# Layer 1's folded ConvFFN: seven-product pairs in a fixed order, with the next pair's weights made between the products

## The chip, the cores and the metric

The kernel runs on one core of one Trainium2 chip. A core has TensorE (PE in the profile, with its weight loads shown as PEld), VectorE (DVE), ScalarE (ACT), GpSimd (POOL) and SyncE (SP), each with an instruction stream of its own that it works through in order; DMA queues are fed from SP and POOL. The metric is the device time of one execution in microseconds (us), as the median over several runs. Lower is better.

## The reference

A decoder trunk of two layers on x of 512 tokens by 1024 channels, in float32. Each layer has a token mixer (layer 0: retention with 4 heads, layer 1: mLSTM with 4 heads) and then a ConvFFN; each of them works on a normed and modulated h and is added to the residual x under a gate. The part that matters here is the ConvFFN:

```python
def causal_dwconv(x, w, b):
    ...
    out = b + xp[:, 0:S] * w[0]
    for j in range(1, K):
        out = out + xp[:, j:j + S] * w[j]

def conv_ffn(h, w_up, conv_w, conv_b, w_down):
    u = causal_dwconv(h @ w_up, conv_w, conv_b)
    a, b = jnp.split(u, 2, axis=-1)
    return (jax.nn.silu(a) * b) @ w_down
```

h is 512 x 1024, w_up 1024 x 5632, the convolution has 3 taps, a and b are 2816 wide each, and w_down is 2816 x 1024.

## The kernel before

Everything is kept with channels on the 128 partitions and the 512 tokens along the free dimension, so x is 8 tiles of 128 x 512 and h likewise. To get float32 accuracy, every operand is split into a high part (a rounded copy, type fp32r) and a low part (what is left over), and each product is three matmuls: high by high, high by low, low by high. For a weight tile of 128 x 1024 (8 k-blocks of 128 columns) the high part is a cast on ACT (`high_part`, L153) and the low part a subtraction on DVE (`low_part`, L158). `low_part_added` makes the low part in another way: ACT writes the negated high part (L164), and a DMA issued from POOL adds the raw weights to it in flight (L165).

Work is listed as `items`, each with the weight chunks that it uses. A planner at the end of the kernel goes through the items in order, and makes chunks (load, high part, low part) up to AHEAD = 4 items ahead, as long as the sum of tiles that are held stays within BUDGET = 20. The wide tiles come from a pool of NWT = 23 slots, and the 128 x 512 tiles from a pool of NSLOTS = 56. Beyond that, a scheduler of the framework fixes the order of the instructions on each engine when the program is built, with the order of the source as priority; on the chip each engine then keeps that order.

The ConvFFN of a layer (class `Ffn`) works on 22 blocks f of 128 channels of a and the same of b. A plain block is two `proj_item`s, 24 matmuls of 512 columns each. The results go through `conv` (ACT and DVE), the gate (silu, product), and a split into the pair `gg`. The down-projection comes in groups of blocks, [4, 4, 4, 4, 6] for layer 1; a group of 4 has 4 pieces of two output tiles, 12 matmuls of 512 columns a tile, and `add_residual` (L377) adds each tile to x. The last group is worked in two halves of 256 tokens (`boundary`), beside the squares for the final norm.

In layer 1 the blocks f = 3 to 21 are folded: the 1024 x 256 weights of a block's pair and h are taken as 2 x 2 blocks (the a and b weights, the two halves of the 8 k-blocks; the two halves of the tokens), and the product is made with seven block products in place of eight (a scheme of Winograd's). `Start.sums` and `Start.turn` make the sums of h once, for all folds. `Fold` makes the sums of the weights of one pair: of the loaded tiles a and b come s13 (two sums on POOL, L187 and L189) and s24 (two on DVE, L188 and L190), then high and low parts of a, s13, s24 and of one half of b (`bp`, L199 and L200). `fold_item` runs the seven products, each 12 matmuls of 256 columns (L315 to L317), into the banks px and py, and combines them: ACT copies three partial results to SBUF (L320, L322, L324), POOL adds two of them there (L325, L328), and three additions on DVE write PSUM (L327, L331, L332). A `Fold` counts 8 tiles in the planner's budget, and each fold is one item; the down pieces of a group stand as items of their own, two after a fold, once the group's blocks are done.

Of the kernel before, what the change touches and what calls it, by code (L numbers as in the profile page):

```python
# [9 lines left out]
F32 = mybir.dt.float32  # L10
# [5 lines left out]
P = 128  # L16
# [11 lines left out]
NWT = 23  # L28
BUDGET = 20
# [8 lines left out]
NSLOTS = 56  # L38
# [30 lines left out]
def trunk(ctx: ExitStack, tc: tile.TileContext, xT, cb, pos, vec, decay, zmask, ada, w_s0, w_in0, w_v0,  # L69
# [107 lines left out]
    class Fold:  # L177


        tiles = 8  # L180

        def __init__(self, src, n, off):
            a, b, s13, s24 = (wide(uid(s)) for s in ("wa", "wb", "ws", "wt"))
# [3 lines left out]
            G.tensor_tensor(f(s13, 0), f(b, 0), f(b, 1), op=ALU.add)  # L187
            V.tensor_tensor(f(s24, 0), f(s13, 0), f(a, 0), op=ALU.subtract)  # L188
            G.tensor_tensor(f(s13, 1), f(a, 0), f(b, 0), op=ALU.subtract)  # L189
            V.tensor_tensor(f(s24, 1), f(a, 1), f(s24, 0), op=ALU.subtract)  # L190
            r = slice(0, n)
# [6 lines left out]
            bp = wide(uid("wb"), F32R)[:, off : off + n]  # L198
            A.copy(f(bp, 0), f(b, 1))  # L199
            V.tensor_tensor(f(bp, 1), f(b, 1), f(bp, 0).bitcast(F32), op=ALU.subtract)  # L200
            self.p = {1: (ah, 0, al, 0), 2: (ah, T, al, T), 3: (s24h, T, s24l, T), 4: (bp, 0, bp, T),
                      5: (s13h, 0, s13l, 0), 6: (s24h, 0, s24l, 0), 7: (s13h, T, s13l, T)}
# [100 lines left out]
    def fold_item(srcs, h, terms, thens):  # L303

        def fn(w):
            p, x_, y_ = w[0].p, bank("px"), bank("py")
            s, q = slot("fs"), slot("fq")

            def product(i, o, start):
# [8 lines left out]
            product(1, x_[:, HA], True)  # L318
            product(6, y_[:, HA], True)
            A.copy(s[:, HA], x_[:, HA])  # L320
            product(5, x_[:, HB], False)
            A.copy(s[:, HB], y_[:, HA])  # L322
            product(7, y_[:, HA], False)
            A.copy(q[:, HA], x_[:, HB])  # L324
            G.tensor_tensor(q[:, HA], q[:, HA], s[:, HA], op=ALU.add)  # L325
            product(2, x_[:, HA], False)
            V.tensor_tensor(y_[:, HB], y_[:, HA], q[:, HA], op=ALU.add)  # L327
            G.tensor_tensor(s[:, HB], s[:, HB], s[:, HA], op=ALU.add)  # L328
# [6 lines left out]
        item([Use(srcs, KT * P, Fold, OFF)], fn)  # L335
# [43 lines left out]
    def contract_tiles(w, n, gate, ys, i, t0, t1, after=lambda m: None):  # L379

        r = slice(t0, t1)
        per = WCOLS // (n * P)
        for j in range(per):
            m = i * per + j
            ps = bank("po")
            for k in range(n):
                cs = slice((j * n + k) * P, (j * n + k) * P + P)
                mm3(ps[:, r], w.hi[:, cs], w.lo[:, cs], ys(k).hi[:, r], ys(k).lo[:, r], k == 0, k == n - 1)
            add_residual(ps, m, gate(m), t0, t1)
            after(m)  # L390

    def pieces(src, n, gate, ys):
# [3 lines left out]
        def piece(i):  # L396
            def run(w, t0, t1, after=lambda m: None):
                contract_tiles(w, n, gate, ys, i, t0, t1, after)
            return Use(src(i), per * n * P), run
# [293 lines left out]
    class Ffn:  # L693
# [31 lines left out]
        def up(self, f):  # L725
            th, w = self.pair(f), w_up[self.layer]
            if self.folded and f > 2:
                fold_item((w[f], w[f + FT]), self.h, self.start.terms, (th, th))
            else:
                proj_item(w[f], self.h, th)  # L730
                proj_item(w[f + FT], self.h, th)
# [6 lines left out]
        def items(self, norm):  # L738
            groups = GROUPS[self.layer]
            if self.folded:  # L740
                ready, gi, end = [], 0, groups[0]
                for f in range(2, FT):
                    self.up(f)
                    if f == 2:
                        item([], lambda w: self.start.turn())
                    if f > end and gi < len(groups) - 1:
                        ready += self.down(gi)
                        gi += 1
                        end += groups[gi]
                    contract_items(ready[:2])  # L750
                    ready = ready[2:]
                contract_items(ready)
# [400 lines left out]
    at, held = 0, []  # L1153
    for n, (uses, fn, free) in enumerate(items):
        held = [u for u in held if u.last >= n]
        while at < len(flat) and (flat[at].first <= n + AHEAD) and (
                sum(u.kind.tiles for u in held) + flat[at].kind.tiles <= BUDGET):
# [3 lines left out]
        fn([u.chunk for u in uses])  # L1161
# [107 lines left out]
```

## Time and profile before

| | |
|---|---|
| median of 3 runs | 1622.29 us (1620.37 to 1623.98) |
| the profiled execution | 1618.41 us, its span 1616.6 us |
| PE busy | 1549.6 us, 96% |
| DVE busy | 1147.1 us, 71% |
| ACT busy | 763.1 us, 47% |
| POOL busy | 265.8 us, 16% |
| mean granted clock of TensorE | 0.988 |

The span runs from the first to the last instruction. A busy time is the time in which an engine had an instruction in work; PE's matmuls overlap, so that the distance between their starts says more than their durations. In rows of groups the columns are line, engine, operation, output and input tiles, shapes and count, then busy us and mean ns of one, then the idle time of the engine just before and what ended it. In rows of waits they are who waited, for whom, us in total, times, longest. In a timeline they are start and duration in us, with idle time before the instruction in brackets. The folded blocks lie between 1262 and 1580 us of the span, and the last down group follows to 1606.

### The profile page before, as it was taken

How to read it: one execution, taken by the hardware profiler on the slowest of the kernel's cores; microseconds unless marked ns; L12 is line 12 of the kernel's file. 1: busy time of each engine (PE TensorE's matmuls, PEld its weight loads, DVE VectorE, ACT ScalarE, POOL GpSimd, SP SyncE). 2: the span in 40 equal slices, each digit the busy share in tenths (PEclk: the TensorE clock that was granted, in tenths of full speed). 3: DMA queues.
4: the chain of work that ended last, by engine and by line, in shares of the span. 5: the costliest groups of instructions: out<-in, count | busy, mean ns of one | idle time of the engine just before them, and what ended most of it. 6: DMA issues, size and time to landing. Idle time of an engine off the chain costs nothing. (4 is left out here: it accounts for less than half of the span.)

```text
span 1616.6 us, 21716 instructions
## 1 busy us (share of the span) xinstructions
PE 1549.6 (96%) x8500; PEld 1340.9 (83%) x8500; DVE 1147.1 (71%) x1616; ACT 763.1 (47%) x1147; POOL 265.8 (16%) x266
## 2 busy tenths in 40 slices
PE   7899999999899999999999999999999798998997
PEld 4688888888888887788988888888898688988887
DVE  8975776777787677763676776757579676776866
ACT  4434524344453243441464554545434656656554
POOL 4221010200110000000110111010204143424322
PEclk9999999999999999999999999999999899999999
DMA  9344446443245655333214232312223455656551
GB/s 364 120 150 142 149 146 214 156 169 127 92 145 175 210 188 182 119 102 104 93 65 131 91 105 66 117 66 91 79 69 79 128 131 148 178 153 170 146 146 52
DMA packets 65304, 216.52 MB, mean 134 GB/s; under 512 B 8993, under 2 KB 11297, under 8 KB 65202
## 3 DMA queue, kind: packets, MB, share of 16 engines
q1 hardware_dynamic: 59730, 195.22, 36.1%
q0 software_dynamic: 5472, 19.93, 6.7%
q8 instruction: 66, 1.08, 0.3%
q14 instruction: 36, 0.29, 0.1%
HBM read 193.06 MB, written 2.12 MB: 121 GB/s over the span
## 5 line engine op out<-in xcount | busy, mean ns | idle before, releaser
L158 DVE TENSOR_TENSOR wlo<-raw,whi 128x1024 fp32r<-128x1024 f32 (+1 forms) x220 | 268.9, 1225 | 84.5 <-ACT whi L153 82.3
L215 PE MATMUL pp<-hh,wlo 128*128 128x512 f32 x800 | 312.4, 390 | 2.7 <-DVE wlo L158 2.7
L213 PE MATMUL pp<-hh,whi 128*128 128x512 f32 x800 | 311.4, 389 | 1.0 <-DVE vl L210 1.0
L214 PE MATMUL pp<-hl,whi 128*128 128x512 f32 x800 | 311.4, 389 | 0.0
L153 ACT CAST whi<-raw 128x1024 fp32r<-128x1024 f32 (+1 forms) x220 | 223.9, 1028 | 77.8 <-DMA raw<-w_in 29.9
L215 PEld LDWEIGHTS pp<-hh,wlo 128*128 128x128 f32 x800 | 150.2, 188 | 37.8 <-DVE wlo L158 6.9
L213 PEld LDWEIGHTS pp<-hh,whi 128*128 128x128 f32 x800 | 150.1, 188 | 32.0 <-DVE vl L210 1.4
L214 PEld LDWEIGHTS pp<-hl,whi 128*128 128x128 f32 x800 | 150.2, 188 | 31.0
L377 DVE SCALAR_TENSOR_TENSOR x<-po,mod,x 128x512 f32<-128x512 f32 (+1 forms) x168 | 102.6, 619 | 91.7 <-PE po L215 91.1
L213 PE MATMUL po<-ggh,whi 128*128 128x512 f32 (+1 forms) x464 | 155.7, 338 | 2.1 <-ACT ggh L209 1.9
L215 PE MATMUL po<-ggh,wlo 128*128 128x512 f32 (+1 forms) x464 | 155.8, 337 | 0.7 <-DVE wlo L158 0.6
L214 PE MATMUL po<-ggl,whi 128*128 128x512 f32 (+1 forms) x464 | 155.8, 337 | 0.0
L215 PE MATMUL po<-yh,wlo 128*128 128x256 f32 (+1 forms) x352 | 116.3, 333 | 3.9 <-DVE wlo L158 3.9
L213 PE MATMUL po<-yh,whi 128*128 128x256 f32 (+1 forms) x352 | 116.6, 332 | 0.8 <-ACT whi L153 0.8
L214 PE MATMUL po<-yl,whi 128*128 128x256 f32 (+1 forms) x352 | 116.4, 331 | 0.0
L130 DVE SCALAR_TENSOR_TENSOR ada<-ada,c_ext 128x1025 f32<-128x1025 f32 x93 | 114.6, 1237 | 0.0
L213 PEld LDWEIGHTS po<-ggh,whi 128*128 128x128 f32 x464 | 87.1, 189 | 12.3 <-ACT ggh L209 2.8
L315 PE MATMUL px<-hh,whi 128*128 128x256 f32 x304 | 87.5, 288 | 9.1 <-ACT whi L153 7.4
L215 PEld LDWEIGHTS po<-ggh,wlo 128*128 128x128 f32 x464 | 87.1, 188 | 10.8 <-DVE wlo L158 1.5
L214 PEld LDWEIGHTS po<-ggl,whi 128*128 128x128 f32 x464 | 87.3, 188 | 8.8
L317 PE MATMUL px<-hh,wlo 128*128 128x256 f32 x304 | 86.8, 286 | 7.4 <-DMA wlo<-wa 7.4
L708 DVE SCALAR_TENSOR_TENSOR cv<-pp,vecs,cv 128x511 f32<-128x511 f32 (+1 forms) x84 | 62.4, 748 | 43.7 <-ACT cv L706 42.6
(285 smaller groups left out, 3420.6 us busy)
## 6 DMA issues: line engine op xcount, KB each, us to landing
ada<-ada SPq DMA_DIRECT2D x96, 512.5 KB, 3.8
raw<-w_in SPq DMA_DIRECT2D x62, 512.0 KB, 3.4
raw<-w_up SPq DMA_DIRECT2D x50, 512.0 KB, 3.3
raw<-w_o SPq DMA_DIRECT2D x32, 512.0 KB, 3.5
raw<-w_dn SPq DMA_DIRECT2D x32, 512.0 KB, 3.4
raw<-w_v SPq DMA_DIRECT2D x28, 512.0 KB, 3.3
wa<-w_up SPq DMA_DIRECT2D x19, 512.0 KB, 3.2
wb<-w_up SPq DMA_DIRECT2D x19, 512.0 KB, 5.4
```

Source lines behind the costliest of these rows:

```text
L130: return V.scalar_tensor_tensor(raw, raw, 1.0, c_ext[:], op0=ALU.mult, op1=ALU.mult, accum_out=mods[layer][:, f : f + 1])
L153: A.copy(hi, w[:, r])
L158: V.tensor_tensor(lo, w[:, r], hi.bitcast(F32), op=ALU.subtract)
L213: PE.matmul(o, ah, bh, start=start, stop=False)
L214: PE.matmul(o, ah, bl, start=False, stop=False)
L215: PE.matmul(o, al, bh, start=False, stop=stop)
L315: PE.matmul(o, hi[:, ch], b[0], start=st, stop=False, skip_group_check=True)
L317: PE.matmul(o, lo[:, cl], b[0], start=False, stop=sp, skip_group_check=True)
L377: V.scalar_tensor_tensor(x[m][:, r], ps[:, r], gate_col, x[m][:, r], op0=ALU.mult, op1=ALU.add)
L708: V.scalar_tensor_tensor(acc[:, s:], ps[:, : T - s], c(j), acc[:, s:], op0=ALU.mult, op1=ALU.add)
```

## The change

The folds begin at f = 4, so block 3 is plain. PE's instructions within a fold item keep the order of the source (`manual_schedule`). The products' results are kept in two banks, c1 and c2: products 1, 6 and 7 are accumulated in one place of c2, with a copy taken after each, and product 5 starts c1's second half; POOL has no part in the combination any more. The weight sums s13 move from POOL to DVE. The weights of fold i + 1 are made in four steps that stand between the products of fold i (`step_a`: high and low of a, and the sums; `step_b`: s13; `step_c`: s24, its low part by DMA for odd folds and by DVE for even ones; `step_d`: the half of b), and the loads of fold i + 2 stand at its end. Folds 1 to 16 have a down piece each, its two tiles before and after product 7; folds 0 and 17 have none, and another order. Of the limits, NWT becomes 22, NSLOTS 58, BUDGET 16, or 20 while a fold is held, and a `Fold` counts 7.

```diff
-NWT = 23
-BUDGET = 20
+NWT = 22
+BUDGET = 16
+BUDGET_FOLD = 20
+FOLD_FROM = 4
...
-NSLOTS = 56
+NSLOTS = 58
...
     class Fold:
-        tiles = 8
+        tiles = 7
...
+        def load(self, src):
+            self.a, self.b = wide(uid("wa")), wide(uid("wb"))
+            nc.sync.dma_start(self.b[:, :WCOLS], src[1])
+            nc.sync.dma_start(self.a[:, :WCOLS], src[0])
+            self.p = {}
+
+        def both(self, w, low, i, j):
+            r = slice(0, WCOLS)
+            hi = high_part(w, r, OFF)
+            lo = low(w, hi, r, OFF)
+            self.p[i], self.p[j] = (hi, 0, lo, 0), (hi, T, lo, T)
+
+        def step_a(self):
+            a, b = self.a, self.b
             f = lambda t, i: t[:, i * T : i * T + T]
-            nc.sync.dma_start(a[:, :n], src[0])
-            nc.sync.dma_start(b[:, :n], src[1])
-            G.tensor_tensor(f(s13, 0), f(b, 0), f(b, 1), op=ALU.add)
+            self.s13, self.s24 = wide(uid("ws")), wide(uid("wt"))
+            s13, s24 = self.s13, self.s24
+            self.both(a, low_part_added, 1, 2)
+            V.tensor_tensor(f(s13, 0), f(b, 0), f(b, 1), op=ALU.add)
+            V.tensor_tensor(f(s13, 1), f(a, 0), f(b, 0), op=ALU.subtract)
             V.tensor_tensor(f(s24, 0), f(s13, 0), f(a, 0), op=ALU.subtract)
-            G.tensor_tensor(f(s13, 1), f(a, 0), f(b, 0), op=ALU.subtract)
             V.tensor_tensor(f(s24, 1), f(a, 1), f(s24, 0), op=ALU.subtract)
-            ah = high_part(a, r, off)
-            al = low_part_added(a, ah, r, off)
-            s24h = high_part(s24, r, off)
-            s24l = low_part(s24, s24h, r, off)
-            s13h = high_part(s13, r, off)
-            s13l = low_part_added(s13, s13h, r, off)
...
+        def step_b(self):
+            self.both(self.s13, low_part_added, 5, 7)
+
+        def step_c(self, added):
+            self.both(self.s24, low_part_added if added else low_part, 6, 3)
+
+        def step_d(self):
+            bp = wide(uid("wb"), F32R)[:, OFF : OFF + WCOLS]
+            A.copy(bp[:, :T], self.b[:, T:WCOLS])
+            V.tensor_tensor(bp[:, T:], self.b[:, T:WCOLS], bp[:, :T].bitcast(F32), op=ALU.subtract)
+            self.p[4] = (bp, 0, bp, T)
...
-            product(1, x_[:, HA], True)
-            product(6, y_[:, HA], True)
-            A.copy(s[:, HA], x_[:, HA])
-            product(5, x_[:, HB], False)
-            A.copy(s[:, HB], y_[:, HA])
-            product(7, y_[:, HA], False)
-            A.copy(q[:, HA], x_[:, HB])
-            G.tensor_tensor(q[:, HA], q[:, HA], s[:, HA], op=ALU.add)
-            product(2, x_[:, HA], False)
-            V.tensor_tensor(y_[:, HB], y_[:, HA], q[:, HA], op=ALU.add)
-            G.tensor_tensor(s[:, HB], s[:, HB], s[:, HA], op=ALU.add)
-            product(3, x_[:, HB], False)
-            product(4, y_[:, HA], False)
-            V.tensor_tensor(x_[:, HB], x_[:, HB], s[:, HB], op=ALU.add)
-            V.tensor_tensor(y_[:, HA], y_[:, HA], s[:, HA], op=ALU.add)
-            thens[0](x_)
-            thens[1](y_)
+            def u2():
+                A.copy(s[:, HB], c2[:, HA])
+                V.tensor_tensor(c1[:, HA], c1[:, HA], s[:, HA], op=ALU.add)
+
+            def u3():
+                A.copy(q[:, HA], c2[:, HA])
+                V.tensor_tensor(c2[:, HB], c1[:, HB], q[:, HA], op=ALU.add)
+            product(1, c2[:, HA], True)
+            if down:
+                product(5, c1[:, HB], True)
+                A.copy(s[:, HA], c2[:, HA])
+                prepare[0]()
+                product(2, c1[:, HA])
+                product(6, c2[:, HA])
+                u2()
+                prepare[1]()
+                down[1](w[1], 0, T, js=(0,))
+                product(7, c2[:, HA])
+                u3()
+                prepare[2]()
+                down[1](w[1], 0, T, js=(1,))
+            else:
+                product(2, c1[:, HA], True)
+                A.copy(s[:, HA], c2[:, HA])
+                prepare[0]()
+                product(6, c2[:, HA])
+                u2()
+                prepare[1]()
+                product(5, c1[:, HB])
+                product(7, c2[:, HA])
+                u3()
+                prepare[2]()
+            product(4, c2[:, HA])
+            product(3, c1[:, HB])
+            prepare[3]()
+            V.tensor_tensor(c1[:, HB], c1[:, HB], s[:, HB], op=ALU.add)
+            thens[0](c1)
+            thens[1](c2)
+            prepare[4]()
...
+                def steps(i):
+                    if i >= len(folds):
+                        return [lambda: None] * 4
+                    return [folds[i].step_a, folds[i].step_b, lambda: folds[i].step_c(i % 2), folds[i].step_d]
...
+                first = [load(0)] + steps(0) + [load(1)]
...
+                early(first[0])
+                self.up(2, lambda: None)
+                early(first[1])
+                th = self.pair(3)
+                proj_item(w[3], self.h, th)
+                early(first[2], first[3])
+                proj_item(w[3 + FT], self.h, th)
+                early(self.start.turn, first[4], first[5])
+                downs = [p for gi in range(len(groups) - 1) for p in self.down(gi)]
+                for i, fold in enumerate(folds):
+                    th = self.pair(FOLD_FROM + i)
+                    fold_item(fold, self.h, self.start.terms, (th, th), downs.pop(0) if i and downs else None,
+                              steps(i + 1) + [load(i + 2)])
...
+    def limit(held):
+        return BUDGET_FOLD if any(u.kind is Fold for u in held) else BUDGET
...
-        fn([u.chunk for u in uses])
+        with tc.manual_schedule(engines={mybir.EngineType.PE}) if any(u.kind is Fold for u in uses) else ExitStack():
+            fn([u.chunk for u in uses])
```

More of the change, by code (lines that the diff above doesn't have):

```diff
@@ L740, in items, with load, fn, early @@
             if self.folded:
[L741 to L752, printed above, removed]
+                w = w_up[self.layer]
+                folds = [Fold(None, 0, 0) for _ in range(FOLD_FROM, FT)]
+                def steps(i):
+                    if i >= len(folds):
+                        return [lambda: None] * 4
+                    return [folds[i].step_a, folds[i].step_b, lambda: folds[i].step_c(i % 2), folds[i].step_d]
+                def load(i):
+                    def fn():
+                        if i < len(folds):
+                            folds[i].load((w[FOLD_FROM + i], w[FOLD_FROM + i + FT]))
+                    return fn
+                first = [load(0)] + steps(0) + [load(1)]
+                def early(*fs):
+                    item([], lambda w: [f() for f in fs])
+                early(first[0])
[11 more added lines that the diff above has]
+                              steps(i + 1) + [load(i + 2)])
+                assert not downs
                 boundary([], self.down(len(groups) - 1), norm)
```

36 lines of the change are left out of this document (14 added, 22 removed).

## The prediction

> **What bounds the kernel now.** I read the page first, then busy time by stretch, then TensorE's (PE's) waits, then the start times of its matmuls.
>
> ```profile
> span 1616.6 us, 21716 instructions
> PE 1549.6 (96%) x8500; PEld 1340.9 (83%) x8500; DVE 1147.1 (71%) x1616; ACT 763.1 (47%) x1147; POOL 265.8 (16%) x266
> ```
>
> The profiled execution took 1618.41 us, 1.8 more than its span and 3.9 less than the median of the runs, 1622.29.
>
> ```profile
> core 0: us, PE busy (x) PEld busy (x) DVE busy (x) ACT busy (x) POOL busy (x), PEclk, DMA share, GB/s
> 0.00:1250.00 1250.00, 1218.11 (x6167) 1032.70 (x6168) 894.89 (x1247) 552.37 (x830) 146.44 (x146) 0.99 0.40 133
> 1262.00:1295.00 33.00, 22.86 (x150) 20.96 (x148) 21.34 (x33) 20.21 (x33) 7.13 (x7) 0.84 0.47 120
> 1295.00:1580.00 285.00, 269.62 (x1908) 251.38 (x1909) 198.98 (x279) 167.30 (x243) 101.69 (x100) 0.99 0.59 152
> 1580.00:1606.00 26.00, 25.75 (x218) 25.24 (x218) 14.71 (x30) 13.10 (x29) 6.05 (x8) 1.00 0.00 1
> ```
>
> PE bounds every stretch. The folded ConvFFN of layer 1 runs from 1262 to 1606, and its first 33 us have 10.1 us of PE idle. VectorE (DVE) is busy for 220.3 us of 318, ScalarE (ACT) for 187.5. The waits of PE from 1262 to 1606:
>
> ```profile
> PE px L315 <- ACT whi L153: 7.4, 1, 7.4
> PE px L317 <- DMA wlo<-wa: 7.4, 4, 3.5
> PE py L315 <- ACT whi L153: 5.6, 3, 1.9
> PE po L213 <- ACT ggh L209: 1.9, 2, 1.0
> PE py L317 <- DVE wlo L158: 1.5, 2, 0.8
> PE px L315 <- ACT fs L320: 1.4, 3, 0.7
> ```
>
> Together 25.2 us, nearly all for weights of a fold that are not ready. Start times show what else is lost:
>
> ```profile
> 1251.05 0.40 PE L213 MATMUL pp<-hh,whi 128*128 128x512 f32 x1
> ...
> 1261.73 0.39 PE L215 MATMUL pp<-hh,wlo 128*128 128x512 f32 x1
> 1261.95 0.28 PE L315 MATMUL px<-hh,whi 128*128 128x256 f32 x1
> ...
> 1275.19 0.58 PE L315 MATMUL px<-hh,whi 128*128 128x256 f32 x1 [7.42 <-ACT whi L153]
> ...
> 1278.33 0.41 PE L315 MATMUL px<-hh,whi 128*128 128x256 f32 x1
> ...
> 1280.67 0.41 PE L317 MATMUL px<-hh,wlo 128*128 128x256 f32 x1
> ...
> 1298.71 0.28 PE L315 MATMUL px<-hh,whi 128*128 128x256 f32 x1
> ...
> 1301.30 0.28 PE L316 MATMUL px<-hl,whi 128*128 128x256 f32 x1
> ...
> 1341.53 0.38 PE L317 MATMUL px<-hh,wlo 128*128 128x256 f32 x1 [1.09 <-DMA wlo<-wa]
> ...
> 1342.90 0.28 PE L316 MATMUL py<-t24l,whi 128*128 128x256 f32 x1
> ...
> 1605.62 0.28 PE L215 MATMUL po<-ggh,wlo 128*128 128x256 f32 x1
> ```
>
> A 512-column matmul starts every (1261.73 - 1251.05)/47 = 0.2272 us. A 256-column one starts every (1301.30 - 1298.71)/22 = 0.1177, but (1280.67 - 1278.33)/11 = 0.2127 after the 7.42 us gap: half speed. After a gap of 1.09 us it is (1342.90 - 1341.53)/11 = 0.125, not half. So a long stall is paid twice.
>
> From 1261.95 to 1605.62 PE does 19 folds x 84 matmuls of 256 columns, 16 down pieces x 24 of 512, and the last group, 8 tiles x 18 matmuls x 2 halves of 256: 1596 x 0.1177 + 384 x 0.2272 + 288 x 0.1177 = 187.8 + 87.2 + 33.9 = 308.9 us. The stretch takes 343.7. **The loss before is 34.8 us**: 25.2 in the waits above, the rest mostly half speed. That is all the change can win in this stage.
>
> **The change part by part.**
>
> *One fold fewer (FOLD_FROM is 4).* Block 3 goes as two plain projections, 48 x 0.2272 = 10.9 us, in place of 84 x 0.1177 = 9.9: **+1.0 us** on PE.
>
> *Sums on DVE, results added in PSUM.*
>
> ```profile
> L189 POOL TENSOR_TENSOR ws<-wa,wb 128x512 f32<-128x512 f32 x17 | 24.7, 1453 | 0.0
> L187 POOL TENSOR_TENSOR ws<-wb 128x512 f32<-128x512 f32 x17 | 24.3, 1430 | 14.5 <-DMA wb<-w_up 14.5
> L158 DVE TENSOR_TENSOR wlo<-wt,whi 128x1024 fp32r<-128x1024 f32 x17 | 21.3, 1251 | 7.6 <-ACT whi L153 7.6
> L188 DVE TENSOR_TENSOR wt<-ws,wa 128x512 f32<-128x512 f32 x17 | 18.0, 1059 | 5.6 <-POOL ws L187 5.6
> L153 ACT CAST whi<-wa 128x1024 fp32r<-128x1024 f32 x17 | 17.8, 1046 | 0.0
> L190 DVE TENSOR_TENSOR wt<-wa,wt 128x512 f32<-128x512 f32 x17 | 12.6, 743 | 0.2
> L322 ACT COPY fs<-py 128x256 f32<-128x256 f32 x19 | 7.1, 373 | 0.0
> L327 DVE TENSOR_TENSOR py<-py,fq 128x256 f32<-128x256 f32 x19 | 8.2, 430 | 25.7 <-PE py L317 16.9 <-POOL fq L325 5.9 <-POOL fs L328 2.9
> ```
>
> DVE gains 18 x 2 sums of 0.743 (26.7 us) and loses 10 of 19 low parts of the difference tile (12.5): 9 folds now take them by DMA, one fold is gone. L188, the same shape as L190 yet 0.32 us longer, should fall to its time with POOL's sums gone (18 x 0.32 = 5.7). So DVE is busy 220 + 26.7 - 12.5 - 5.7 = 229 us of about 300, ACT about 187 + 9 negations at the cast's 1.05 less the dropped fold's three such = 194. Both lie beside PE: nothing on the path while their queues are in time. The two partial-result additions of POOL go, the three ACT copies and three DVE additions stay; POOL keeps DMA issues alone.
>
> *The order of PE fixed.* One fold with a down piece takes, from its start: products 1, 5, 2, 6 to 5.65 us, a down tile to 8.38, product 7 to 9.79, a down tile to 12.52, products 4 and 3 to 15.34 (1.41 a product, 2.73 a tile). The new wait is product 4's: it writes the bank of product 7, so it needs the copy (0.373) and the addition (0.430) behind product 7. Queued behind it on PE are all products of the next fold. Cover: the 2.73 us tile. With one 1.05 us ACT cast and one 1.25 us DVE subtraction ahead in their in-order queues the chain takes 3.1 us, 0.4 too much; without them 0.8. I take 0.2 for each of 16 folds: **3 us**. Folds 0 and 17 have no down tiles: copy, addition and handover bare, about 1 us each: **2 us**.
>
> *Weights of the next fold in four steps.* Every step starts a fold ahead and waits for what stands before it in program order, not for the slots of a whole fold. The loads of its two tiles are issued a whole fold (15 us) ahead on SP's queue, where today's slower one lands in 5.4:
>
> ```profile
> wb<-w_up SPq DMA_DIRECT2D x19, 512.0 KB, 5.4
> ```
>
> They cost nothing under that cover. The queue that counts is POOL's for the accumulating DMAs, two a fold before, three in the 9 odd folds after:
>
> ```profile
> 1333.54 0.88 POOL L165 DMA_DIRECT2D wlo<-wa  x1
> 1340.92 0.86 POOL L165 DMA_DIRECT2D wlo<-ws  x1 [6.50 <-issue]
> ...
> 1484.67 0.88 POOL L165 DMA_DIRECT2D wlo<-wa  x1 [5.39 <-ACT wlo L164]
> 1488.25 0.86 POOL L165 DMA_DIRECT2D wlo<-ws  x1 [2.70 <-issue]
> ...
> 1506.39 0.89 POOL L165 DMA_DIRECT2D wlo<-wa  x1
> 1510.80 0.87 POOL L165 DMA_DIRECT2D wlo<-ws  x1 [3.52 <-issue]
> ```
>
> From issue to landing they take, by the low parts' own view:
>
> ```profile
> DMA to landing us min/median/max: 4.4/5.2/7.9
> ```
>
> The second issue is held with nothing visible to wait for: 7.38, 3.58 and 4.41 us apart, mean 5.1. So three DMAs occupy the queue for 15.3 us of a 15.34 us fold. The first can go at about 4.2 (product 1, copy, cast, negation), the others at 9.3 and 14.4; the last lands at 14.4 + 5.2 = 19.6. Product 6 of the next fold reads that low part at 15.34 + 4.24 + 0.24 = 19.8. The mean just fits; at 3.58 a step it is 3.2 us early, at 7.38 it is 4.4 late. I take 0.8 for each odd fold, near the mean since the spread goes both ways: **7 us**; ends 0 and 40. [...]
>
> *The start.* Ends: 0, and the 10.1 us idle of today. I take **3 us**, nearer to 0, since the plain pair gives DVE and ACT 10.9 us to get ahead.
>
> *The end.* The last group waits for block 21's gated product (today's row: 1.9 us); tiles of other columns can start before it. **3 us**, ends 0 and 6.
>
> *Tiles.* NWT 22 and BUDGET 16 act on the whole kernel, but going through the planner's rule item by item no item before the folds holds over 16, so nothing is loaded later by plan; 6 spare slots are left there in place of 7 or more. PE's idle before 1250 is 31.9 us, spread out. I take 0; ends -1 and +4.
>
> **Sum.** Loss after: 3 + 2 + 7 + 3 + 3 = 18. 1618.41 - 34.8 + 1.0 + 18 = 1602.6, and with the 3.9 to the median **1606**.
>
> **The rivals.**
> *Nothing is late (1594).* Only the bare chains and the end stay, 6 us: 1618.4 - 34.8 + 1.0 + 6 + 3.9 = 1594. For: DVE at 76% and ACT at 65% have room. Against: the POOL queue's spread.
>
> *The DMA queue decides (slower, 1639).* If each accumulating DMA takes 6.2 us of the queue, the last lands at 4.2 + 12.4 + 6.2 = 22.8, 3 us late in each odd fold, and half speed over some 15 matmuls (0.2127 for 0.1177) adds 1.4 each: 9 x 4.4 = 40 beside the other 11 us: 1618.4 - 34.8 + 1.0 + 51 + 3.9 = 1639. It decides from 2.5 us a fold, 5.9 us a DMA. For: 7.38 in one row. Against: 3.58 and 4.41. [...]
>
> *Product 4's wait decides (slower, 1630).* If ACT does the next cast and negation (2.1) and DVE a subtraction ahead of the copy and addition, the chain is 4.2 us plus handover, 1.7 over the tile: 16 x 1.7 = 27 beside 15: 1618.4 - 34.8 + 1.0 + 42 + 3.9 = 1630. It decides from 1.2 a fold. For: ACT and DVE keep their order whatever is late. Against: both have idle a third and a quarter of the time.
>
> *No change (1622).* The weights wait for tile slots as today, so the 34.8 us stay in another place. A fold needs its 7 tiles, the next one's 6 in the making, a loaded pair and the down pieces' 5: 20 of 22.
>
> **How the numbers follow.** 0.2% (3.2 us) is about what can be told from no change. Chances: forecast 0.48 (its own range 1597 to 1617), nothing late 0.18, queue 0.13, product 4 0.12, no change 0.09. Faster takes the first two, 0.66; same 0.08, most of the last; slower the rest, 0.26. Below 1591 I leave the part of the second where the start also wins; above 1634 most of the queue's case.
>
> **What would show it.** Right: PE's idle in this stage falls below 15 us; waits on L153's casts vanish; the sums on DVE take about 0.74; POOL is busy only with issues; DMA waits of PE sit at product 6 of every second fold. Wrong: PE waits for an addition at product 4 in most folds; POOL issues over 5.9 us apart in threes; PE at half speed again; or idle ahead of the folds grown by more than 4 us.

## The result: 1695 us, slower by 4.5%

The changed kernel takes 1695.22 us (median of 4 runs, 1693.83 to 1696.52), the kernel before beside it 1623.13 (4 runs): a ratio of 1.0446, 95% interval 1.0428 to 1.0464. The forecast was 1606, and slower was given 0.26. The profiled execution took 1694.29 us.

The page of the changed kernel, its span and busy times:

```profile
span 1692.5 us, 21688 instructions
PE 1572.4 (93%) x8464; PEld 1358.7 (80%) x8464; DVE 1140.3 (67%) x1638; ACT 775.2 (46%) x1149; POOL 185.0 (11%) x197
```

Busy time by stretch of the changed kernel, with the columns of the same view of before:

```profile
0.00:1250.00 1250.00, 1220.44 (x6194) 1035.17 (x6195) 895.50 (x1260) 555.92 (x836) 137.94 (x141) 0.99 0.38 133
...
1295.00:1580.00 285.00, 226.48 (x1404) 207.19 (x1404) 150.12 (x229) 141.16 (x190) 28.41 (x33) 0.89 0.52 134
```

Little moved before the folds. Inside them, from 1295 to 1580, PE began 1404 matmuls where it was 1908, and the granted clock fell from 0.99 to 0.89. VectorE and ScalarE are idle more than before, so no engine has become the bound.

TensorE's waits from 1250 us on, in the changed kernel:

```profile
PE p L334 <- ACT fs L348: 69.9, 16, 7.0
PE p L336 <- DMA wlo<-ws: 6.1, 1, 6.1
PE p L334 <- DVE p L344: 5.0, 3, 2.4
```

The waits for casts are gone. One new wait holds nearly everything: 16 times, once in each fold with a down piece, a product waits for the copy in line 348. That is **product 6**, whose 12 matmuls add to the place in c2 where product 1's result lies, so that they may begin only when the 0.37 us copy `A.copy(s[:, HA], c2[:, HA])` has read it.

How much is lost in all? PE's timeline of the changed kernel, the start and the end of the stage:

```profile
1267.76 0.28 PE L334 MATMUL p<-hh,whi 128*128 128x256 f32 x1
...
1681.58 0.28 PE L236 MATMUL pms<-ssh,ones_d 128*128 128x256 f32 x1
```

413.8 us for 18 folds x 84 matmuls, 384 of 512 columns and 288 of 256, which at the distances found in the trace of before take 1512 x 0.1177 + 384 x 0.2272 + 288 x 0.1177 = 299.1. The loss has gone from 34.8 us to 114.7: 81.0 in waits and 33.7 in slower matmuls, most of it at half speed behind the waits (at a granted clock of 0.50 PE is busy for 61.7 us of the stage, of which some 28 are lost at 0.2127 us a matmul for 0.1177). The span grew by 80 for that loss, less 9.9 for the fold that is gone, plus 5.8 because the folds start that much later: 75.9, which is 1692.5 - 1616.6.

Now the copy itself. One fold of the changed kernel, ScalarE's timeline:

```profile
1375.22 1.05 ACT L155 CAST whi<-wt 128x1024 fp32r<-128x1024 f32 x1 [1.46 <-DMA wlo<-wa]
...
1377.90 1.45 ACT L748 ACTIVATE cv<-p,vecs 128x512 f32<-128x512 f32 x2 [1.11 <-DVE p L373]
1380.88 0.63 ACT L760 ACTIVATE cv<-cv 128x512 f32<-128x512 f32 x1 [1.53 <-DVE cv L750]
1382.28 0.62 ACT L227 CAST ggh<-cv 128x512 fp32r<-128x512 f32 x1 [0.76 <-DVE cv L761]
1383.18 1.04 ACT L155 CAST whi<-raw 128x1024 fp32r<-128x1024 f32 x1 [0.29 <-DMA raw<-w_dn]
1384.13 0.36 ACT L348 COPY fs<-p 128x256 f32<-128x256 f32 x1
```

PE's timeline around it, with the matmuls behind the wait:

```profile
1375.19 0.28 PE L334 MATMUL p<-hh,whi 128*128 128x256 f32 x1
...
1377.80 0.28 PE L336 MATMUL p<-hh,wlo 128*128 128x256 f32 x1
1384.55 0.58 PE L334 MATMUL p<-t24h,whi 128*128 128x256 f32 x1 [6.47 <-ACT fs L348]
1384.93 0.41 PE L335 MATMUL p<-t24l,whi 128*128 128x256 f32 x1
...
1387.06 0.41 PE L336 MATMUL p<-t24h,wlo 128*128 128x256 f32 x1
```

The row at 1375.19 is the first of product 5, so product 1, just ahead of it, is done by about 1375.5; 1377.80 is the last of product 2. The copy starts at 1384.13. In ScalarE's order it stands behind the whole gate of the block before: convolution (L748), silu (L760), the cast of the product (L227), with VectorE's half (L750, L761) between them, so that ScalarE itself waits for much of the time (1.53 and 0.76 us here). In this fold it also stands behind the cast of the next down piece (L155, whi<-raw), which waits for its load. The rows show that ScalarE keeps to this order: the copy's input had been ready for over 8 us, in which ScalarE stood idle for 3.7 us (1.11, 1.53, 0.76 and 0.29) and did not take the copy first.

In seven folds the cast stands ahead too, and the gap is 4.9 to 7.0 us; in seven others it is 2.5, with the gate alone; the first two have 6.3 and 3.7. The cast and its wait are only a part of the difference, because in the seven long cases the gate also begins late. VectorE's timeline of the changed kernel, the addition L373 that opens the gate, in a long case and in the short one behind it:

```profile
1376.30 1.23 DVE L160 TENSOR_TENSOR wlo<-wt,whi 128x1024 fp32r<-128x1024 f32 x1 [2.78 <-ACT whi L155]
1377.44 0.43 DVE L373 TENSOR_TENSOR p<-p,fs 128x256 f32<-128x256 f32 x1
...
1398.20 0.43 DVE L373 TENSOR_TENSOR p<-p,fs 128x256 f32<-128x256 f32 x1 [2.08 <-PE p L336]
```

In the short case the addition begins as soon as PE is done with product 3. In the long one VectorE's subtraction for wt stands ahead of it and waits for a cast, so that it begins 3.6 us behind the start of product 1 (1.5 to 4.0 in the seven). The two kinds take turns, as `step_c` makes that low part on VectorE for every second pair only. And behind the long gap PE runs at half speed: (1387.06 - 1384.93)/10 = 0.213 us a matmul.

The chain of waits over these folds of the changed kernel shows why the load is late:

```profile
1360.49 6.23 DMA raw<-w_dn
...
1370.65 4.46 DMA wlo<-wa
1375.22 1.06 ACT whi L155
...
1377.44 0.43 DVE p L373
1377.87 0.60 DVE wb L219
1378.49 4.62 DMA raw<-w_dn
...
1384.13 0.37 ACT fs L348
```

It is a ring. The down piece's cast lets ScalarE get to the cast and negation of wa; the accumulating DMA of wa's low part reads wa, and the cast of wt waits for it (8.9 us in 7 waits); VectorE's subtraction for wt, in front of the addition L373, and step d follow; then the piece's load is issued, and its cast stands ahead of the copy. What is late in one fold makes the next one late.

Before the tests there were three theories. **A, the queue:** the copy's place on ScalarE behind the gate chain costs the time. **A', the piece:** the cast of the late down piece ahead of the copy costs it, and the gate is only a part. **B, the order:** that PE's order is fixed costs it, since PE could do other products meanwhile. A rival **C** was that there are too few tile slots, so that weights are late, and the prediction's rival, the DMA queue, was kept beside them.

### The profile page after: what moved, and what is told of

Its sections match the earlier page's. It is cut to its first block, busy times and chain, and to the rows that moved or that the text cites. A ratio compares the mean times of both kernels' runs of the same rounds, so it can differ in the third digit from the quotient of the medians.

```text
span 1692.5 us, 21688 instructions
## 1 busy us (share of the span) xinstructions
PE 1572.4 (93%) x8464; PEld 1358.7 (80%) x8464; DVE 1140.3 (67%) x1638; ACT 775.2 (46%) x1149; POOL 185.0 (11%) x197
## 4 chain that ended last, share of the span: by engine, by line
PE 69%; DVE 11%; DMA 9%; issue 7%; ACT 4%; SPq 0%; POOL 0%; DVEq 0%; ACTq 0%; POOLq 0%
PE pp L233 10%; PE pp L232 10%; PE pp L231 10%; PE po L231 6%; PE po L233 6%; PE po L232 6%; DMA raw<-w_dn 4%; PE pv L407 3%; PE pv L406 3%; PE pv L408 3%; DMA wlo<-wa 2%; DVE wlo L160 2%; DMA wlo<-ws 2%; ACT whi L155 2%; DVE cv L750 1%
## 5 line engine op out<-in xcount | busy, mean ns | idle before, releaser
L233 PE MATMUL pp<-hh,wlo 128*128 128x512 f32 x816 | 318.6, 391 | 2.6 <-DVE wlo L160 2.6
L232 PE MATMUL pp<-hl,whi 128*128 128x512 f32 x816 | 317.6, 389 | 0.0
L231 PE MATMUL pp<-hh,whi 128*128 128x512 f32 x816 | 317.4, 389 | 0.0
L155 ACT CAST whi<-raw 128x1024 fp32r<-128x1024 f32 (+1 forms) x222 | 226.3, 1029 | 103.2 <-DMA raw<-w_dn 44.8
L231 PE MATMUL po<-ggh,whi 128*128 128x512 f32 (+1 forms) x464 | 161.5, 351 | 0.1
L232 PE MATMUL po<-ggl,whi 128*128 128x512 f32 (+1 forms) x464 | 161.1, 348 | 0.0
L233 PE MATMUL po<-ggh,wlo 128*128 128x512 f32 (+1 forms) x464 | 159.7, 345 | 0.6 <-DVE wlo L160 0.6
L231 PEld LDWEIGHTS po<-ggh,whi 128*128 128x128 f32 x464 | 91.0, 197 | 10.1 <-ACT ggh L227 0.3
L232 PEld LDWEIGHTS po<-ggl,whi 128*128 128x128 f32 x464 | 91.1, 196 | 9.1
L750 DVE SCALAR_TENSOR_TENSOR cv<-pp,vecs,cv 128x511 f32<-128x511 f32 (+1 forms) x88 | 65.4, 748 | 43.9 <-ACT cv L748 42.6
L334 PE MATMUL p<-t24h,whi 128*128 128x256 f32 x72 | 27.9, 388 | 69.9 <-ACT fs L348 69.9
L336 PE MATMUL p<-hh,wlo 128*128 128x256 f32 x288 | 81.8, 284 | 6.1 <-DMA wlo<-ws 6.1
```

The costliest lines, as they stand in the source:

```text
L155: A.copy(hi, w[:, r])
L231: PE.matmul(o, ah, bh, start=start, stop=False)
L232: PE.matmul(o, ah, bl, start=False, stop=False)
L233: PE.matmul(o, al, bh, start=False, stop=stop)
L336: PE.matmul(o, lo[:, cl], b[0], start=False, stop=sp, skip_group_check=True)
L750: V.scalar_tensor_tensor(acc[:, s:], ps[:, : T - s], c(j), acc[:, s:], op0=ALU.mult, op1=ALU.add)
```

## Experiments

The kernel before, run beside them, took 1620.9 to 1623.8 us. All but the kernel with the best parts together were run once each. Six runs of the kernel before spread over 6.3 us (1618.24 to 1624.56), so differences of tens of us are clear, and those under some 6 are not.

### PE's order left to the scheduler

```diff
-        with tc.manual_schedule(engines={mybir.EngineType.PE}) if any(u.kind is Fold for u in uses) else ExitStack():
-            fn([u.chunk for u in uses])
+        fn([u.chunk for u in uses])
```

> Edit: PE's fixed source order inside a fold is taken away, all else as in the changed kernel (1695 us). Theory A (ScalarE's order: the short copy of product 1's result stands behind the previous fold's gate chain and behind the cast of the next down piece, and product 6 waits for it, 69.9 us in 16 folds plus half speed): the copy stays late, but a free order can put down tiles into the gap, so some of the 72 us comes back: 1640 to 1675. Rival B (the fixed PE order itself is the cause, other queues are fine): all of it comes back, 1600 to 1625. Rival C (too few tile slots, weights late): hardly any change, over 1680.

1681.62 us. TensorE's waits of this kernel:

```profile
PE p L336 <- DMA wlo<-ws: 39.3, 11, 6.1
PE p L336 <- DMA wlo<-wa: 19.5, 6, 4.8
PE p L334 <- ACT fs L348: 4.6, 1, 4.6
```

The wait for the copy nearly goes, 13.6 us are won, and some 70 us of waits remain, 58.8 of them now for low parts. The order alone (B) isn't the cause. Theory A's 1640 to 1675 was missed too; the time lies where C had put it, with weights that come late, as the ring has them.

### The gate chain behind the copy

The conv and gate of a fold (`thens`) are kept back and put behind the copy of the next fold, in the source and in ScalarE's order.

```diff
+            def behind(cp):
+                with tc.issue_after(cp.ins):
+                    while waiting:
+                        waiting.pop(0)()
...
-                A.copy(s[:, HA], c2[:, HA])
+                cp = A.copy(s[:, HA], c2[:, HA])
+                behind(cp)
...
-            thens[0](c1)
-            thens[1](c2)
+            gate = lambda: (thens[0](c1), thens[1](c2))
+            if last:
+                gate()
+            else:
+                waiting.append(gate)
```

> Edit: conv and gate of the previous fold are traced behind the first copy of the fold and queued behind it on ScalarE; nothing else. Theory A: product 6's wait of 69.9 us falls below 10, and half speed goes with it: 1600 to 1630. Rival D (the wait only moves: the second copy, behind product 6, now stands behind silu and casts, and product 7 waits for it): PE waits of 30 to 60 us at product 7, 1640 to 1680. Rival C (slots): product 6 then waits for weights, over 1680.

**1606.59 us**, 88.6 less. TensorE's waits of this kernel:

```profile
PE p L338 <- DMA wlo<-ws: 13.5, 9, 6.8
PE p L338 <- DMA wlo<-wt: 3.8, 1, 3.8
```

No wait for the copy is left, none of product 7 has come in its place (rival D), and the cast of the down piece holds PE up once, for 0.5 us. This undoes the whole loss without touching anything that the change adds. But two things have moved: beside the gate, the scheduler has now put the piece's cast behind the copy, in 15 of 16 folds. ScalarE's timeline of this kernel:

```profile
1382.62 0.37 ACT L354 COPY fs<-p 128x256 f32<-128x256 f32 x1 [3.96 <-PE p L338]
...
1384.23 1.05 ACT L155 CAST whi<-raw 128x1024 fp32r<-128x1024 f32 x1
```

### Only the piece's cast behind the copy, and both

```diff
             nc.sync.dma_start(raw[:, r], src)
+            if in_folds[0]:
+                waiting.append(lambda: self.split(raw, r, off))
+            else:
+                self.split(raw, r, off)
+
+        def split(self, raw, r, off):
             self.hi = high_part(raw, r, off)
             self.lo = low_part(raw, self.hi, r, off)
```

> Edit: only the high and low part of the next down piece are queued behind the first copy, the gate chain stays ahead of it. Theory A with both causes: the long waits of every second fold (5 to 7 us, the cast waits for the piece's load) fall to the short kind (2.8 us), the short ones stay: product 6 waits 40 to 50 us in total, 1640 to 1665. If the gate chain alone counts: no change, 1690 to 1700. If the cast alone counts: 1600 to 1630.

> Edit: gate chain and cast of the next down piece both queued behind the first copy. Theory A: product 6's wait below 10 us, 1600 to 1625, at or a little below the run of the gate chain alone. Rival D: as there, product 7 waits instead, 1640 to 1680.

1626.37 us with the cast alone behind the copy, 1609.18 with both. The first missed the range of theory A with both causes and lies in that of the cast alone. So the cast ahead of the copy is worth 68.9 us while the gate stays ahead. In that run PE still waits for the copy, but only 13.9 us in 13 times, and the gate ahead of it costs 17.2 us (1626.37 - 1609.18) where gate and cast together cost 86.0 (1695.22 - 1609.18). The 1609.18 has nearly the order of the second experiment, where the cast was behind already, and the 2.6 us between them say nothing. What the cast ahead costs once the gate is behind is left to a run below.

### The piece's load ahead of the pair's

If the late load is the trouble, issue it first: on SP's queue it stands behind wb and wa of the next pair, and wa waits for a slot (in the changed kernel 41.6 us in 7 waits for the accumulating DMA that still reads ws).

```diff
+            prepare[4]()
             product(1, c2[:, HA], True)
...
             thens[1](c2)
-            prepare[4]()
...
-                              steps(i + 1) + [load(i + 2)])
+                              steps(i + 1) + [load(i + 1)])
```

> Edit on the changed kernel: the load of the next down piece stands ahead of the loads of the next pair on SyncE's queue (the pair's loads are traced at the start of the next fold); ScalarE's order is left to the scheduler as in the changed kernel. Theory A': the cast of the piece is late since its load stands behind a load that waits for a tile slot; with the load early the cast no longer waits, product 6's waits shrink as in the run with the cast behind: 1625 to 1650. If the load's place on SyncE's queue doesn't matter: 1685 to 1700.

1698.68 us: a miss, in the range for a place that doesn't matter. SyncE's waits of this kernel:

```profile
SPq L175 <- PE p L336: 190.8, 16, 17.7
...
SPq L189 <- DMA wlo<-ws: 32.1, 6, 6.4
```

The load (L175) has become first in its queue, and now it waits for a tile slot itself. The order on SP's queue was not what made it late; slots that come free late are. Most of these waits are for PE's products, which still read the tiles, and some are for the accumulating DMAs.

### The gate behind, the cast ahead

The counterpart that separates A from A': as the second experiment, but the copy is queued behind the piece's cast.

```diff
             self.hi = high_part(raw, r, off)
+            piece_cast[0] = casts[-1]
...
-                cp = A.copy(s[:, HA], c2[:, HA])
+                with tc.issue_after(piece_cast[0].ins):
+                    cp = A.copy(s[:, HA], c2[:, HA])
```

> Edit on the run with the gate chain behind (1606.6): the copy is queued behind the cast of the next down piece, which the scheduler had put behind it there. So cast ahead, gate behind: the counterpart of the run with gate ahead, cast behind (1626.4). Theory A' (the cast, which waits for its late load, is the larger cause): product 6 waits 30 to 70 us again, 1640 to 1685. If it is the gate chain that counts: 1605 to 1615.

1598.80 us, below both ranges, with no wait for the copy in PE's list. A' falls: the cast ahead of the copy does no harm of its own, and with the gate alone behind it 96.4 us of the 1695.22 are gone. The gate ahead is what every large loss needs; the cast ahead makes it larger. The 7.8 us below the second experiment are little for single runs. The cast still waits for its load (21.3 us in 11 waits), but now in time that ScalarE has to spare.

### Low parts off the accumulating DMA, and the sums back on POOL

Both with the gate behind the copy.

```diff
-            self.both(self.s13, low_part_added, 5, 7)
+            self.both(self.s13, low_part, 5, 7)
```

> Edit on the run with the gate chain behind (1606.6): the low part of the sum tile s13 is made by VectorE's subtraction, not by an accumulating DMA. There PE still waits 17.6 us for the DMAs of low parts, 13.5 of them at product 5 for s13's. If these DMAs are what is left: 1585 to 1598, waits on DMA below 5 us. If VectorE becomes late in their place (it gains 18 x 1.2 us): 1600 to 1615.

```diff
-            V.tensor_tensor(f(s13, 0), f(b, 0), f(b, 1), op=ALU.add)
-            V.tensor_tensor(f(s13, 1), f(a, 0), f(b, 0), op=ALU.subtract)
+            G.tensor_tensor(f(s13, 0), f(b, 0), f(b, 1), op=ALU.add)
+            G.tensor_tensor(f(s13, 1), f(a, 0), f(b, 0), op=ALU.subtract)
```

> Edit on the run with the gate chain behind (1606.6): the two sums of s13 go back to GpSimd. If the move of the sums to VectorE is part of the gain: s13 and with it the DMA of its low part come 1.5 to 2 us later, product 5 waits longer, 1610 to 1630. If it doesn't matter: within 3 us of 1606.6.

1594.17 and 1611.22 us. With VectorE making s13's low part, the waits for it go and 12.4 us with them; some 10 us of short waits are left, 8.3 of them for DMAs, where below 5 had been expected. With the sums on POOL the time is 4.6 longer, too little for single runs, and product 5 doesn't wait longer, as the range for a gain had required (11.9 us for ws, 13.5 before): that the move of the sums gains anything is not shown.

### The best parts together

```diff
+                with tc.issue_after(piece_cast[0].ins):
+                    cp = A.copy(s[:, HA], c2[:, HA])
+                behind(cp)
...
-            self.both(self.s13, low_part_added, 5, 7)
+            self.both(self.s13, low_part, 5, 7)
```

> The two best of the edits together: the gate chain behind the copy of product 1, the copy behind the cast of the next down piece (1598.8 alone), and the low part of s13 by a subtraction on VectorE (1594.2 alone). If the gate chain ahead of the copy is the whole of what was lost and the late low parts the rest, the two gains (7.8 and 12.4 us over the 1606.6 with the gate chain behind) add up in part, since both take from the same 17.6 us of waits for low parts: 1584 to 1597, faster than before by 1.5 to 2.4 per cent, and no wait of product 6. If they conflict (VectorE's subtraction is in the queue with the sums that the cast ahead of the copy delays), 1597 to 1610.

**1587.60 us** (4 runs, 1587.10 to 1587.74) against 1620.86 for the kernel before (6 runs): a ratio of 0.979, 95% interval 0.9766 to 0.9815. It beats both kernels; whether by 2% or more over the one before, the interval leaves open. TensorE's longest wait of this kernel, and two rows of its timeline:

```profile
PE p L341 <- DVE wlo L162: 1.8, 1, 1.8
```

```profile
1269.60 0.28 PE L339 MATMUL p<-hh,whi 128*128 128x256 f32 x1
...
1574.64 0.28 PE L239 MATMUL pms<-ssh,ones_d 128*128 128x256 f32 x1
```

The stage takes 305.0 us for 299.1 of work: a loss of 5.9, where it was 34.8 before and 114.7 in the changed kernel.

### The copy on VectorE

Back to the changed kernel, with the gate ahead: does it matter on which engine the copy stands?

```diff
-                A.copy(s[:, HA], c2[:, HA])
+                V.tensor_copy(s[:, HA], c2[:, HA])
...
```

> As the changed kernel, but product 1's result is copied by VectorE and not by ScalarE, so that neither the gate's cast nor the cast of the next down piece stands ahead of it; VectorE's own part of the gate (two operations that wait for ScalarE) still may. Theory (the queue in which the copy stands costs the time): the copy comes at the end of VectorE's gate work, in the trace of the changed kernel some 2 us earlier than now, and product 6 waits under 1 us in most folds: 1605 to 1640. Rival (the copy itself, or the bank that it shares with products 1 and 6, is what product 6 waits for, on whichever engine): 1685 to 1705 with the wait still in 16 folds.

1691.30 us: a miss. VectorE's timeline of this kernel, one fold:

```profile
1382.13 2.73 DVE L750 SCALAR_TENSOR_TENSOR cv<-p,vecs,cv 128x511 f32<-128x511 f32 x4 [0.26 <-ACT cv L748]
...
1386.34 0.69 DVE L228 TENSOR_TENSOR ggl<-cv,ggh 128x512 fp32r<-128x512 f32 x1 [0.68 <-ACT ggh L227]
1386.95 0.42 DVE L348 COPY fs<-p 128x256 f32<-128x256 f32 x1
```

PE still waits for the copy, 64.4 us in 16 times, at least 3.3 in every fold. The gate runs over both engines, and VectorE's end of it (L228) comes after ScalarE's. I had counted on the piece's cast no longer being in front; with the whole gate in front, and one operation more of it, that wins nothing. It is not ScalarE that must be avoided but the place behind the gate. That the wait would stay on either engine had been my rival's number, though for another reason, a cost of the copy or of the bank; the second experiment, where copy and bank are as they were and the wait is gone, rules that out.

### The gate behind, PE's order free

The second experiment with the first one's edit added.

> The gate chain behind the copy, as in the run that gave 1606.6, but TensorE's order left to the scheduler. Theory (the order of TensorE is not what costs, the late copy is): within 8 us of 1606.6, since with the copy on time the written order has little left to wait for but the low parts. Rival (the written order keeps TensorE waiting where it could go on): 1585 to 1597, with the waits for low parts down to under 8 us.

1603.82 us, 2.8 from 1606.59: with the copy in time the fixed order costs little or nothing that single runs can show.

### The gate ahead, fewer accumulating DMAs

The changed kernel with the low parts of s13 and of every s24 made on VectorE.

```diff
-            self.both(self.s13, low_part_added, 5, 7)
+            self.both(self.s13, low_part, 5, 7)
...
-            self.both(self.s24, low_part_added if added else low_part, 6, 3)
+            self.both(self.s24, low_part, 6, 3)
```

> As the changed kernel, with the gate chain still ahead of the copy, but the low parts of both sums by subtractions on VectorE; only product 1's stays an accumulating DMA. Theory (the copy's place in ScalarE's queue): product 6 still waits in most folds, 50 us and more, 1660 to 1705. Rival (the accumulating DMAs share the transfer engines with the loads, and make the loads late that the casts wait for): the wait for the copy falls below 30 us, 1600 to 1640.

1637.42 us, in the rival's range, though the wait for the copy, 38.2 us, lies between the two. TensorE's wait for the copy in this kernel, then product 6's start in one fold:

```profile
PE p L334 <- ACT fs L348: 38.2, 16, 7.4
```

```profile
1349.03 0.39 PE L334 MATMUL p<-t24h,whi 128*128 128x256 f32 x1 [1.88 <-ACT fs L348]
```

This run does not test the DMAs alone. The scheduler has put the piece's cast behind the copy in 15 of 16 folds, where it stood ahead in seven, and that alone had given 1626.4 with all the DMAs kept. So it isn't shown which of the two brings the 57.8 us (1695.22 - 1637.42). What it does show is the gate by itself: the down piece's load comes in time (ScalarE waits 11.0 us for it in place of 33.6), the ring is cut, and in 13 of 16 folds the gap is the same 1.88 us. From product 3's end to the copy's start lie the addition (0.43), the convolution's three steps, silu, product and cast, in the changed kernel's rows above from 1377.44 to 1382.90, 5.5 us; the copy takes 0.36; against it stand products 1, 5 and 2, 3 x 1.41 = 4.2 us. 5.5 + 0.4 - 4.2 = 1.7, close to the 1.88 found.

So the 1695.2 us come apart only roughly. With the ring cut the gate ahead of the copy costs 43.2 us here (1637.4 against 1594.2, where the gate is behind; the low parts of half the s24 also differ between these two) and 17.2 in the run with the cast behind. With the gate behind, the accumulating DMA of s13 costs 12.4. All together cost 101 us (1695.2 - 1594.2); the 45 us or more that are in none of these fit the feedback, the long gaps and the half speed behind them, but no run measures that share by itself.

Not tried: product 1 in a bank of its own, or more tile slots. Rival C is answered only so far: with the gate behind, the same 22 slots give 1599 to 1607, so their number alone is not the cause. Open is also how much of the 1691 us with the copy on VectorE is the ring's share.

## Why the prediction was wrong

**The step that failed is "The order of PE fixed".** It read the fixed order for handovers in one bank, found product 4's ("The new wait is product 4's"), and gave it 3 us for 16 folds and 2 for two more. That wait is there, 5.0 us in all, but in 3 folds and not in 18: the total agrees by luck. But the same argument holds for product 6, which adds to the bank of product 1. It was never priced: its 2.8 us of cover (products 5 and 2) look ample for a 0.37 us copy, if one counts only the copy. The step counted one cast and one subtraction ahead of the copy behind product 7. For product 1's copy it should have counted all that stands there, and what that waits for: the gate's chain over two engines. The runs put 69.9 us of waits in its place, with half speed behind them, and moving that one chain behind the copy takes 96.4 us off while the piece's cast stays ahead (1598.80).

**"Nothing on the path while their queues are in time"** held the failure in its last words. The additions, the sums and the gate were judged by busy time (VectorE 229 us of 300, 9 more than before). Busy time was no trap: over the whole stage VectorE's fell, from 235.0 us to 226.5. ScalarE, busy for 141 of 285 us between 1295 and 1580, was late in 16 of 18 folds, since its order put a short operation that PE needs behind long ones that PE needs later.

**"They cost nothing under that cover"**, the loads issued a whole fold ahead: wrong in what they hold up. In the changed kernel wa's load was held for slots 41.6 us in 7 waits, and the piece's load behind it (issued at 1378.49 in the chain above, its cast at the front of ScalarE's queue at 1382.9). The count of 20 slots of 22 left out that an accumulating DMA keeps its source tile until it lands: those 41.6 us are waits for the DMA that reads ws, which lands 6.3 us behind its issue in the median.

**The accumulating DMAs.** "7 us" was for PE waiting at product 6 for a low part; PE waited 6.1 us, once, at the start. With the gate behind it is 17.3 us with the start's, for 7 + 3 given. The spacing assumed, 5.1 us an issue, did not hold: with the gate behind two issues stand 2.3 us apart. Landing took longer instead, 6.5 us in the median where it was 5.2, and 8.8 at most; the fastest landing in the changed kernel is 4.4. The low parts' own view of the gate-behind kernel, and POOL's timeline:

```profile
DMA to landing us min/median/max: 4.5/6.5/8.8
```

```profile
1345.02 0.86 POOL L167 DMA_DIRECT2D wlo<-ws  x1 [3.00 <-ACT fq L345]
1347.32 0.86 POOL L167 DMA_DIRECT2D wlo<-wt  x1 [1.44 <-ACT wlo L166]
```

The rival of the DMA queue was right that these DMAs cost time (1594.2 without s13's, for 1606.6), and wrong on the place: in the changed kernel they delay slots and casts (waits of 41.6 and 8.9 us), and through them PE.

**What held.** The sums take 0.68 to 0.69 us on VectorE, for 0.74 said; POOL only issues; the waits for casts are gone; the start has one wait of 6.1 us, for 3 with ends 0 and 10.1; the last group shows no wait, for 3 (the 0.4 us wait behind it is for the final norm's squares, as before); block 3 put the folds later by 5.8 us, of which 10.9 are its two plain projections, so some 5 were won ahead of them, outside the ends of -1 and +4 given. "The loss before is 34.8 us", all that can be won, stands as a bound: the best version has 5.9 left. And 1606 is close to what the change gives with the copy in time (1606.6), where 25 us are lost (1593.89 - 1269.64 - 299.1, the stage's ends there) for 18 foreseen, in part an accident of terms that cancel.

**The signs.** PE's idle in the stage, said to fall below 15 us, was 81, and PE's one wait for a DMA was at the start. Of the four signs named as "wrong" half speed came, and POOL's issues did stand over 5.9 us apart in seven of the nine threes, though by a wait for ScalarE's negation and not by the queue (10.2 us from 1343.58 to 1353.73). None of the four looked at product 6's copy.

The third rival, product 4's wait, had what ruled here ("ACT and DVE keep their order whatever is late": the copy above stood ready for over 8 us) and set it at the wrong product.

## What to carry to other kernels

When matmuls reuse a PSUM place after a copy, list for every such copy what stands ahead of it in its engine's queue, and follow each entry to the engine that it waits for; here entries that hop between two engines took 5.5 us ahead of a copy of 0.37. Put work that TensorE needs next ahead of work that it needs a fold later, and look for rings: a tile slot freed by a late DMA, which delays a load, which delays a cast in the same queue. Two delays in one ring can cost more than their sum, and mending either one may bring most of it back: here 86.0 us for gate and cast together, 17.2 for the gate alone, nothing for the cast alone.

## What was not expected of the hardware

The clock fell after gaps much shorter than the long ones, and with a delay. PE's timeline of the changed kernel, two folds in which product 6 begins behind the same gap (at 1404.92 and 1448.60):

```profile
1404.92 0.39 PE L334 MATMUL p<-t24h,whi 128*128 128x256 f32 x1 [2.52 <-ACT fs L348]
...
1406.80 0.63 PE L232 MATMUL po<-ggl,whi 128*128 128x512 f32 x1
...
1409.36 0.62 PE L232 MATMUL po<-ggl,whi 128*128 128x512 f32 x1
...
1448.60 0.38 PE L334 MATMUL p<-t24h,whi 128*128 128x256 f32 x1 [2.53 <-ACT fs L348]
...
1450.08 0.40 PE L231 MATMUL po<-ggh,whi 128*128 128x512 f32 x1
...
1452.60 0.39 PE L233 MATMUL po<-ggh,wlo 128*128 128x512 f32 x1
```

The same two places by stretches of 3.41 us, with the columns of the views above (PE's busy time first, the granted clock behind POOL's):

```profile
1403.03:1406.44 3.41, 1.52 (x13) 1.52 (x14) 1.95 (x4) 0.89 (x2) 0.00 (x0) 1.00 1.02 250
1406.44:1409.85 3.41, 3.41 (x11) 2.67 (x10) 0.00 (x0) 1.02 (x2) 0.00 (x0) 0.50 0.60 231
1443.99:1447.40 3.41, 2.08 (x18) 1.87 (x16) 3.41 (x6) 1.47 (x3) 0.15 (x1) 1.00 1.00 234
1447.40:1450.82 3.42, 2.22 (x16) 2.09 (x17) 1.26 (x3) 1.26 (x3) 0.00 (x0) 1.00 1.00 213
```

After the gap that ends at 1404.92 PE runs at full speed for 1.5 us, then at half, (1409.36 - 1406.80)/6 = 0.427 us for 512 columns, for about 3.4 us. After the equal gap that ends at 1448.60 it never slows: (1452.60 - 1450.08)/11 = 0.229. From the folds on, the changes of the granted clock in this trace, from 1276.73 us to 1686.33, lie within 0.05 us a whole number of 3.413 us from the first. The first gap puts 1.89 us of idle (3.41 - 1.52) into one stretch, and the clock is 0.50 in the next; the second is cut in two, 1.33 and 1.20, and nothing follows. So what counts is how the gap falls into these stretches. Over the folds, each of the 13 stretches at full clock in which PE idles for 2.09 us or more has 0.50 behind it, and none of those with 1.58 or less has; of the two between, 1.89 is followed by 0.50 and 1.93 by 1.00. In the run with fewer accumulating DMAs a gap of 1.88 us was enough: the matmuls behind the one that ends at 1349.03 slowed as well, (1353.66 - 1350.67)/7 = 0.427 us for 512 columns, for some 3 us. The gap of 1.09 us in the trace of before, which kept the speed, agrees with this.
